# Hybrid mLSTM / sliding-window decoder layer: the forget gates' rows placed behind a branch gate's weights, and two value-projection weights whose remainders come from adding transfers

## The chip, the core and the metric

The kernel runs on one core of a Trainium2 chip. The metric is the device time of one execution in microseconds (us): the median of three runs was 878.63 us (878.37 to 880.06). One further execution was taken with the hardware profiler; all rows below come from it. Times inside the program are counted from the start of the profile's span.

The engines are named as the profile names them: PE is the matrix engine, PEld its weight load, DVE the vector engine, ACT the scalar engine, POOL the engine that here mostly issues transfers, SP the engine that issues most loads from memory. A row such as "L138 DVE TENSOR_TENSOR wl<-wr,wh" is an instruction of line 138 that reads the tiles wr and wh and writes the tile wl.

## The reference

One decoder layer over 512 tokens of width 1024, all in float32. What matters here is the first third of it:

```python
h = rmsnorm(x, norm_mix_g[i])
proj = h @ w_in[i]
qk_ml, v_ml, o_ml, if_pre, q_sw, k_sw, v_sw, g_a, g_b = jnp.split(proj, split_idx, axis=-1)
...
gates = (if_pre + b_if[i]).astype(jnp.float32)
ig = gates[..., :ML_HEADS]
lf = jax.nn.log_sigmoid(gates[..., ML_HEADS:])
h_ml = mlstm_chunkwise(q_ml, k_ml, v_ml.reshape(B, S, ML_HEADS, ML_DV), ig, lf)
...
y_a = jax.nn.sigmoid(o_ml) * h_ml
y_b = swa_with_sinks(...)
merged = jax.nn.sigmoid(g_a) * (y_a @ w_branch_a[i]) + jax.nn.sigmoid(g_b) * (y_b @ w_branch_b[i])
x = x + merged @ w_out[i]
```

A squared-ReLU MLP, a gated per-layer embedding and a last norm follow. `v_ml` is the value projection of the mLSTM, `o_ml` its output gate, `g_b` and `g_a` the two branch gates, `lf` the logarithm of the forget gates (four heads by 512 tokens), and `mlstm_chunkwise` runs over running sums and running maxima of `lf` and `ig`.

## The kernel before

**Two parts of each number.** A float32 operand of a matmul is split into a rounded part, `wh`, and a remainder, `wl`; a product is then three matmuls, written by `pairs` in the order high·high, high·low, low·high. For a weight this happens in `load_w`: a raw tile `wr` (128x1024, 512 KB) is cast by ACT to `wh` (L137) and DVE subtracts `wh` from `wr` into `wl` (L138). There are four buffers each for `wr`, `wh` and `wl`; a buffer of `wh` or `wl` comes free when PE has done the products of the weight four earlier, a buffer of `wr` when its last reader is done, and SP's next load into it waits for that. Where a later row of the projection's own raw tiles is not in `wr` it is in a tile called `wq`.

**Splitting by a transfer.** `split_by_transfer` does the same with DVE left out: ACT casts the high part (L145), ACT writes the negative of the rounded raw data into the low part's place through a scaled copy (L146), and POOL issues a transfer that adds the raw data onto it (L147). Before the change it is used only for sums of activations, tiles `hS`, 256 KB each.

**Seven products instead of eight.** Value projection, output gate and both branch gates are computed by `seven`, a scheme that forms a 2x2 block product from seven block products. Its products run in this order, with the results that each completes: p1, c11, t21, t22, c22, c12, c21. Before each, `form` splits a weight; some weights are first added to or subtracted from each other on DVE (L452, L453, L462, L466). `post` reads the accumulated result (ACT copies p1; DVE adds t21 and t22, at L515 or L646). In value projection and output gate (`by_tokens`) a product has two weights, 24 matmuls of 512 columns; in the branch gates (`gate_proj`, run twice for each gate, j = 0 and 1) it has one weight, 24 matmuls of 256 columns. Accumulators of a product pair are reused: t22 adds to t21's, so PE waits for DVE to have read t21; c11 adds to p1's, so PE waits for ACT's copy of p1.

**Order.** Every engine works through its own queue strictly in the order in which its instructions stand. Tile's scheduler merges the parts of the program into those queues by its own estimates; `tc.issue_after` and a few other calls hold a part behind a named instruction. The stages around the change are, in PE's order: value projection (44 to 83 us), output gate (83 to 122 us), first branch gate `w_gb` (122 to 164 us).

**The gates' rows.** `gates()` works on the four-partition rows of the input and forget gates: DVE L583, ACT exponential L584, ACT logarithm L585, DVE L586 together give `lf`; then a running maximum `mst` (L588), four running sums `fl` (L591), `rr` (L593), seven steps of `gg` (L600, L602), and one more exponential `em` on ACT (L604). The functions belong to different ACT tables, so table loads (ACT_TABLE_LOAD) stand between them. `gates` is called when the first branch gate's t22 is posted, but in the program as built L583 to L591 stand much earlier, within the value projection. The transposes of these rows (`gate_columns`) follow in the second half of the first branch gate.

Of the kernel before, what the change touches and what calls it, by code (L numbers as in the profile page):

```python
# [13 lines left out]
ALU = mybir.AluOpType  # L14
# [22 lines left out]
def block_kernel(  # L37
# [30 lines left out]
    V, A, G, T = nc.vector, nc.scalar, nc.gpsimd, nc.tensor  # L68
# [63 lines left out]
    last_low = [None]  # L132
# [19 lines left out]
        nc.sync.dma_start(out=raw[:, :n], in_=src)  # L152
        return raw

    def load_w(src, n, dims, raw=None, cast=False):

        if raw is None:
            raw = load_raw(src, n)
        parts = [wp.tile([P, 1024], F32R, tag=t, bufs=WB, name=nm(t))[:, :n] for t in ("wh", "wl")]
        if cast:  # L160
            nc.gpsimd.dma_start(out=parts[0], in_=src)
            last_low[0] = V.tensor_sub(parts[1], raw[:, :n], r32(parts[0]))
        else:
            split(parts, raw[:, :n])
        return [q.rearrange("p (k c) -> p k c", k=dims) for q in parts]

    def pairs(a, b):
# [215 lines left out]
    A11, A12, A22 = h_part(1, 1), h_part(1, 2), h_part(2, 2)  # L383
# [55 lines left out]
        S3.extend(h_split(s3))  # L439
        S4.extend(h_split(s4))  # L440

    def seven(form, prod, X, Y, Z, b, post, own_first=False):

        b11, b12, b21, b22 = b
        n = range(len(b11))
        for i in n:
            prod(X, A11, form(b11[i]), i, True)
        post("p1", X)  # L450
        for i in n:
            V.tensor_sub(b12[i], b22[i], b12[i])  # L452
            V.tensor_add(b11[i], b12[i], b11[i])  # L453
        for i in n:
            prod(X, A12, form(b21[i]), i, False, True)
        own = last_mm[0].ins
        if own_first:
            with tc.issue_after(last_low[0].ins):
                late_sums()
        post("c11", X)  # L460
        for i in n:
            V.tensor_sub(b21[i], b21[i], b11[i])  # L462
            w = form(b11[i])
            with tc.issue_after(own) if own_first else ExitStack():
                prod(Z, S2, w, i, True)
            V.tensor_sub(b11[i], b22[i], b11[i])  # L466
        post("t21", Z)
        for i in n:
            prod(Z, S1, form(b11[i]), i, False)
        post("t22", Z)  # L470
        for i in n:
            prod(Y, S3, form(b12[i]), i, True)
        post("c22", Y)
        for i in n:
            prod(Z, S4, form(b22[i]), i, False, True)
        post("c12", Z)
        for i in n:
            prod(Y, A22, form(b21[i]), i, False, True)
        post("c21", Y)


# [4 lines left out]
        vm.append(t)  # L486
    vld = dp.tile([P, NH, NT, DV], F32, name="vld")

    def by_tokens(w, post, own_first=False):

        raws = quads(w, ["wr", "wr", "lm", "lm", "wr", "wr", "lm", "lm"])
        b = ps_a()
        X, Y, Z = [ps_t(), ps_t()], [b[:, :512], b[:, 512:]], [ps_g(), ps_g()]

        def prod(ps, f, w, kh, first, last=False):
            for t in range(2):
                ops = []
                for k in range(2):
                    ops += pairs([h[:, t * P : (t + 1) * P] for h in f[2 * kh + k]], [h[:, k, :] for h in w])
                chain(ps[t], ops, first and kh == 0, last and kh == 1, True)  # L500

        seven(lambda r: load_w(None, 1024, 2, r), prod, X, Y, Z, [raws[2 * i : 2 * i + 2] for i in range(4)], post, own_first)

    def post_by_tokens(done):

# [40 lines left out]
    for m in range(NT):  # L546
        T.transpose(pgi[:4, m * P : (m + 1) * P], gt[:, m, :4], ident)
        T.transpose(pgf[:4, m * P : (m + 1) * P], gt[:, m, 4:], ident)
    by_tokens(w_vml, post_by_tokens(put_v), True)
    store_low()  # L550


# [27 lines left out]
    def gates():  # L580

        lf = row("lf")[:4, :]
        V.scalar_tensor_tensor(lf, fg, -1.0, fg, ALU.mult, ALU.max)  # L583
        A.activation(lf, lf, AF.Exp, scale=-1.0)  # L584
        A.activation(lf, lf, AF.Ln, bias=1.0)  # L585
        V.scalar_tensor_tensor(lf, fg, 0.0, lf, ALU.min, ALU.subtract)  # L586
        mst = act_f("mst")[:4, :]
        V.tensor_tensor_scan(mst, lf, ig, 0.0, ALU.add, ALU.max)  # L588
        fl = row("fl")[:4, :]
        for c in range(NT):  # L590
            V.tensor_tensor_scan(fl[:, c * P : (c + 1) * P], lf[:, c * P : (c + 1) * P], zeros4, 0.0, ALU.add, ALU.add)  # L591
        rr = act_f("rr")[:4, :]
        V.tensor_sub(rr, fl, mst)  # L593

        rrd = dp.tile([NH, 512], F32, name="rrd")
        nc.gpsimd.dma_start(out=rrd, in_=rr)
        gg = [act_f("gg")[:4, :] for _ in range(NT)]
        for t in range(NT):
            sl = slice(t * P, (t + 1) * P)
            V.tensor_sub(gg[t][:, sl], ig[:, sl], fl[:, sl])  # L600
            if t:
                V.tensor_scalar_add(gg[t][:, : t * P], gg[t - 1][:, : t * P], fl[:, t * P - 1 : t * P])  # L602
        em = act_f("em")[:4, :]
        A.activation(em, mst, AF.Exp, scale=-1.0)  # L604
        rows.extend(row("row") for _ in range(NH))
        for h in range(NH):
            nc.gpsimd.dma_start(out=rows[h], in_=rrd[h : h + 1, :].broadcast_to([P, 512]))
        rows_of_gates.extend((gg, em))
# [887 lines left out]
```

## Time and profile before

| | |
|---|---|
| median of three runs | 878.63 us |
| lowest and highest run | 878.37, 880.06 us |
| the profiled execution, its time | 878.13 us |
| its span, first to last instruction | 876.3 us |
| matmuls, whole span | 4428 |
| PE idle or late between 66 and 77 us / 77 and 89 / 124 and 137 / 137 and 151 | 0.00 / 0.35 / 0.42 / 0.00 us |
| bytes read from memory and written to it | 97.60 MB, 10.49 MB |

The row on idle time is the length of each stretch less PE's busy time in it. In a timeline a row gives start, duration, engine, line, operation, what is written and read, and in square brackets how long the engine was idle before it and what ended that. Rows of one line that follow each other directly are merged ("x2"): the start is that of the first. A duration includes the pipeline's end, so the next instruction can start a little before it is over.

### The profile page before, as it was taken

The page shows a single profiled execution, that of the slowest core. Times are in us where ns is not written, and L with a number is a line of the kernel's source. Part 1 is how long each engine was busy: PE and PEld are TensorE (multiplying, and loading weights), DVE is VectorE, ACT ScalarE, POOL GpSimd, SP SyncE. Part 2 cuts the span into 40 slices and gives each one's busy share as a digit, 9 for nine tenths or more (in the row PEclk, how much of TensorE's full clock was granted, in tenths as well). Part 3 has the DMA queues.
Part 4 walks back from the last instruction along what each step waited for, and adds up shares of the span by engine and source line. Part 5 has one row for each costly group of instructions (what it writes and reads, how often), then busy time and mean ns, then how long its engine had stood idle before and what let it go on. Part 6 is the DMA issues. An engine that isn't in the chain of part 4 may idle for free.

```text
span 876.3 us, 11735 instructions
## 1 busy us (share of the span) xinstructions
PE 864.2 (99%) x4428; PEld 727.1 (83%) x4428; DVE 671.5 (77%) x994; ACT 490.4 (56%) x826; POOL 43.7 (5%) x70
## 2 busy tenths in 40 slices
PE   9999999999999999999999999999999999999996
PEld 7888789998877778888888888888888888888886
DVE  6999889775788889777896669757956784698557
ACT  6685556444676568854344665356435634564843
POOL 1121111000000000000020000000000000020000
PEclk9999999999999999999999999999999999999999
DMA  8775246435121266664244612520452054125302
GB/s 268 209 185 207 97 148 209 146 115 202 49 97 50 72 231 215 209 254 148 73 88 148 222 47 73 204 106 4 135 178 73 0 192 145 49 54 139 120 1 96
DMA packets 35162, 115.14 MB, mean 131 GB/s; under 512 B 4893, under 2 KB 4893, under 8 KB 35106
## 3 DMA queue, kind: packets, MB, share of 16 engines
q1 hardware_dynamic: 28146, 95.25, 31.5%
q0 software_dynamic: 6816, 18.89, 7.9%
q8 instruction: 35, 0.57, 0.3%
q10 hardware_dynamic: 144, 0.26, 0.1%
q14 instruction: 21, 0.17, 0.1%
HBM read 97.60 MB, written 10.49 MB: 123 GB/s over the span
## 4 chain that ended last, share of the span: by engine, by line
PE 84%; DVE 7%; ACT 4%; DMA 3%; issue 2%; SPq 0%; ACTq 0%; DVEq 0%
PE psg L175 47%; PE psp L175 23%; PE psa L175 5%; DVE wl L138 2%; PE pst L175 2%; PE pst L778 1%; ACT wh L137 1%; DMA wr<-in_w_vsif 1%; DMA wq<-in_w_o 1%; ACT lm L743 1%; PE psa L720 1%; PE psa L859 1%; PE psa L881 1%; DVE qs L429 1%; PE psa L879 1%
## 5 line engine op out<-in xcount | busy, mean ns | idle before, releaser
L137 ACT CAST wh<-wr 128x1024 fp32r<-128x1024 f32 x130 | 136.5, 1052 | 159.4 <-PE psg L175 61.7
L138 DVE TENSOR_TENSOR wl<-wr,wh 128x1024 fp32r<-128x1024 f32 x130 | 158.1, 1219 | 79.9 <-ACT wh L137 78.9
L175 PE MATMUL psg<-x,wh 128*128 128x512 f32 x512 | 157.7, 389 | 0.0
L175 PE MATMUL psp<-wh,uf 128*128 128x512 f32 x448 | 138.5, 389 | 0.0
L175 PEld LDWEIGHTS psg<-x,wh 128*128 128x128 f32 x512 | 96.1, 188 | 19.9
L175 PE MATMUL psg<-x,wl 128*128 128x512 f32 x256 | 99.6, 389 | 0.0
L175 PEld LDWEIGHTS psp<-wh,uf 128*128 128x128 f32 x448 | 84.1, 188 | 17.4
L175 PE MATMUL psp<-wl,uf 128*128 128x512 f32 x224 | 87.1, 389 | 0.0
L175 PE MATMUL psg<-h,wh 128*128 128x512 f32 x256 | 80.9, 395 | 0.6 <-DVE rc L746 0.6
L137 ACT CAST wh<-wd 128x1024 fp32r<-128x1024 f32 x44 | 46.2, 1052 | 54.1 <-PE psp L175 21.9
L138 DVE TENSOR_TENSOR wl<-wd,wh 128x1024 fp32r<-128x1024 f32 x44 | 53.1, 1218 | 14.6 <-ACT wh L137 14.5
L175 PEld LDWEIGHTS psg<-x,wl 128*128 128x128 f32 x256 | 48.1, 188 | 9.9
L175 PEld LDWEIGHTS psg<-h,wh 128*128 128x128 f32 x256 | 46.9, 188 | 11.2 <-issue 1.6
L175 PE MATMUL psg<-h,wl 128*128 128x512 f32 x128 | 50.5, 395 | 0.0
L138 DVE TENSOR_TENSOR uf<-F,uf 128x1792 fp32r<-128x1792 f32 (+2 forms) x20 | 33.0, 1652 | 21.8 <-ACT uf L137 21.8
L175 PEld LDWEIGHTS psp<-wl,uf 128*128 128x128 f32 x224 | 42.1, 188 | 8.9
L175 PE MATMUL psg<-yb,wh 128*128 128x512 f32 x128 | 40.3, 393 | 0.0
L175 PE MATMUL psg<-ya,wh 128*128 128x512 f32 x128 | 39.9, 391 | 0.0
L137 ACT CAST uf<-F 128x1792 fp32r<-128x1792 f32 (+2 forms) x20 | 27.9, 1396 | 20.5 <-DVE F L1191 20.4
L1215 DVE SCALAR_TENSOR_TENSOR xk<-psp,r,xk 128x512 f32<-128x512 f32 x48 | 33.8, 744 | 5.5 <-PE psp L175 5.2
L175 PE MATMUL psg<-hS,wh 128*128 128x256 f32 x192 | 35.6, 285 | 0.2 <-DVE t L646 0.2
L175 PE MATMUL psa<-h,wh 128*128 128x256 f32 x192 | 35.4, 285 | 0.3 <-ACT p L656 0.2
(343 smaller groups left out, 1828.4 us busy)
## 6 DMA issues: line engine op xcount, KB each, us to landing
wr<-in_w_up SPq DMA_DIRECT2D x32, 512.0 KB, 3.3
wd<-in_w_down SPq DMA_DIRECT2D x24, 512.0 KB, 4.0
wr<-in_w_qsw SPq DMA_DIRECT2D x8, 512.0 KB, 4.2
gd<-gr POOLq DMA_DIRECT2D x8, 512.0 KB, 2.9
wr<-in_w_qkml SPq DMA_DIRECT2D x8, 512.0 KB, 3.2
wr<-in_w_b SPq DMA_DIRECT2D x8, 512.0 KB, 3.2
wh<-in_w_b POOLq DMA_DIRECT2D x8, 512.0 KB, 3.7
gl<-gd SPq DMA_DIRECT2D x8, 512.0 KB, 4.3
```

The costliest lines, as they stand in the source:

```text
L137: A.copy(dst[0], src)
L138: last_low[0] = V.tensor_sub(dst[1], src, r32(dst[0]))
L175: last_mm[0] = T.matmul(ps, l, r, start=first and i == 0, stop=last and i == len(ops) - 1, skip_group_check=parts)
L429: V.tensor_sub(t[o, :], ps[s, :], r32(t[s, :]))
L720: T.matmul(o, q[:, n * P : (n + 1) * P], kk[kp][ab][:, k0 : k0 + 256], start=True, stop=False)
L743: A.activation(lm3[:, g, :], lm3[:, g, :], AF.Exp, bias=nmx[:, g : g + 1], scale=0.125, accum_out=sm[:, g : g + 1])
L778: T.matmul(o[HALF[ab], :], v[:, c : c + 64], w[:, ab * 512 : (ab + 1) * 512], start=j == 0, stop=j == len(terms) - 1)
L859: T.matmul(psc[s], l, r, start=j == 0, stop=j == 2, skip_group_check=True)
L879: T.matmul(o, hi, vm[s][:, h, :], start=s == 0, stop=False, skip_group_check=True)
L881: last_mm[0] = T.matmul(o, lo, vm[s][:, h, :], start=False, stop=s == t, skip_group_check=True)
L1215: V.scalar_tensor_tensor(o, ps[:, t, :], r2[:, 2 * toks + t : 2 * toks + t + 1], o, ALU.mult, ALU.add)
```

## The change

`seven` gets a `last_form`, used for the two weights of its last product, c21; `by_tokens` makes it from a new argument `how`, and only the value projection passes one, `split_by_transfer`. `load_w` uses `how` in place of `split`. And the first instruction of `gates` is held behind `last_low[0]`, the subtraction that was recorded last when `gates` is called: that of the first branch gate's t22 weight.

```diff
-    def load_w(src, n, dims, raw=None, cast=False):
+    def load_w(src, n, dims, raw=None, cast=False, how=None):
...
-            split(parts, raw[:, :n])
+            (how or split)(parts, raw[:, :n])
...
-    def seven(form, prod, X, Y, Z, b, post, own_first=False):
+    def seven(form, prod, X, Y, Z, b, post, own_first=False, last_form=None):
...
         for i in n:
-            prod(Y, A22, form(b21[i]), i, False, True)
+            prod(Y, A22, (last_form or form)(b21[i]), i, False, True)
         post("c21", Y)
...
-    def by_tokens(w, post, own_first=False):
+    def by_tokens(w, post, own_first=False, how=None):
...
-        seven(lambda r: load_w(None, 1024, 2, r), prod, X, Y, Z, [raws[2 * i : 2 * i + 2] for i in range(4)], post, own_first)
+        seven(lambda r: load_w(None, 1024, 2, r), prod, X, Y, Z, [raws[2 * i : 2 * i + 2] for i in range(4)], post, own_first, lambda r: load_w(None, 1024, 2, r, how=how))
...
-    by_tokens(w_vml, post_by_tokens(put_v), True)
+    by_tokens(w_vml, post_by_tokens(put_v), True, split_by_transfer)
...
         lf = row("lf")[:4, :]
-        V.scalar_tensor_tensor(lf, fg, -1.0, fg, ALU.mult, ALU.max)
+        with tc.issue_after(last_low[0].ins):
+            V.scalar_tensor_tensor(lf, fg, -1.0, fg, ALU.mult, ALU.max)
```

One line is added in `gates`, so from there on a line of the changed kernel has a number higher by one (L583 becomes L584, L646 becomes L647), and the tiles' own numbers rise by two.

ACT's queue at the value projection's last weights, before (`wr_556` and `wr_558` are the two raw weights of c21, `vm` is a result):

```order
L137 CAST wh_792<-wq_560 128x1024
L137 CAST wh_808<-wq_562 128x1024
L137 CAST wh_834<-wr_556 128x1024
L137 CAST wh_850<-wr_558 128x1024
L540 CAST vm_530<-t_140_745 128x2x256
```

and now:

```order
L137 CAST wh_792<-wq_560 128x1024
L137 CAST wh_808<-wq_562 128x1024
L146 ACTIVATE wl_835<-wr_556 128x1024
L145 CAST wh_834<-wr_556 128x1024
L146 ACTIVATE wl_852<-wr_558 128x1024
L145 CAST wh_851<-wr_558 128x1024
L540 CAST vm_530<-t_140_745 128x2x256
```

Two instructions are added on ACT; DVE loses its two subtractions for these weights, and POOL gets two transfers, `wl_835<-wr_556` and `wl_852<-wr_558`, ahead of its third store of `vld`.

DVE's queue in the first branch gate, before, from the subtraction for the c12 weight (`wl_1379`) to that for the weight of the next half's p1 (`wl_1458`); the c21 weight is `wl_1410`:

```order
L138 TENSOR_TENSOR wl_1379<-wr_1178,wh_1378 128x1024
L646 TENSOR_TENSOR t_228_1277<-psg_1183,p_223_1214 128x256
L593 TENSOR_TENSOR rr_1320<-fl_1315,mst_1313 4x512
L600 TENSOR_TENSOR gg_1324<-ig_877,fl_1315 4x128
L600 TENSOR_TENSOR gg_1325<-ig_877,fl_1315 4x128
L602 TENSOR_SCALAR gg_1325<-gg_1324,fl_1315 4x128
L600 TENSOR_TENSOR gg_1326<-ig_877,fl_1315 4x128
L602 TENSOR_SCALAR gg_1326<-gg_1325,fl_1315 4x256
L600 TENSOR_TENSOR gg_1327<-ig_877,fl_1315 4x128
L602 TENSOR_SCALAR gg_1327<-gg_1326,fl_1315 4x384
L138 TENSOR_TENSOR wl_1410<-wr_1176,wh_1409 128x1024
L138 TENSOR_TENSOR wl_1458<-wq_1443,wh_1457 128x1024
```

Now, from the t22 weight (`wl_1283`) to `rr`; behind `rr` come the same seven rows of `gg`, then the subtractions `wl_1412` and `wl_1460` for the c21 weight and the next half's p1 weight:

```order
L138 TENSOR_TENSOR wl_1283<-wr_1174,wh_1282 128x1024
L584 SCALAR_TENSOR_TENSOR lf_1310<-fg_880 4x512
L138 TENSOR_TENSOR wl_1351<-wr_1176,wh_1350 128x1024
L647 TENSOR_TENSOR t_228_1279<-psg_1184,p_223_1216 128x256
L647 TENSOR_TENSOR t_228_1279<-psg_1185,p_223_1216 128x256
L452 TENSOR_TENSOR wq_1447<-wr_1451,wq_1447 128x1024
L587 SCALAR_TENSOR_TENSOR lf_1310<-fg_880,lf_1310 4x512
L589 SCALAR_TENSOR_TENSOR mst_1315<-lf_1310,ig_879 4x512
L592 SCALAR_TENSOR_TENSOR fl_1317<-lf_1310,zero_90 4x128 x4
L138 TENSOR_TENSOR wl_1381<-wr_1180,wh_1380 128x1024
L594 TENSOR_TENSOR rr_1322<-fl_1317,mst_1315 4x512
```

The whole chain of the rows now stands between the c22 weight (`wl_1351`) and the p1 weight (`wl_1460`), and L452, which before stood behind the p1 weight, stands in it as well; before, only `mst`, `rr` and `gg` stood here.

ACT's queue at the same place, now (before, L584 and L585 with their table loads stood in the value projection, and the casts of the c12, c21 and p1 weights followed that of the c22 weight with one sigmoid among them):

```order
L137 CAST wh_1282<-wr_1174 128x1024
L137 CAST wh_1350<-wr_1176 128x1024
L585 ACT_TABLE_LOAD
L585 ACTIVATE lf_1310<-lf_1310 4x512
L668 ACT_TABLE_LOAD
L668 ACTIVATE gr_1186<-psa_1182 128x2x256
L586 ACT_TABLE_LOAD
L586 ACTIVATE lf_1310<-lf_1310 4x512
L137 CAST wh_1380<-wr_1180 128x1024
L137 CAST wh_1411<-wr_1178 128x1024
L137 CAST wh_1459<-wq_1445 128x1024
```

Three table loads stand ahead of the c12 weight's cast, one of them more than the whole program had.

PE's queue where c22 of the first half ends, before (`psa_1181` is c22, `psa_1451` the next half's p1):

```order
L175 MATMUL psa_1181<-hS_652,wl_1349 128x256
L175 MATMUL psa_1451<-h_158,wh_1457 128x256
L175 MATMUL psa_1451<-h_159,wh_1457 128x256
L175 MATMUL psa_1451<-h_158,wl_1458 128x256
L175 MATMUL psa_1451<-h_158,wh_1457 128x256
```

and now (`psa_1183` is c22, `psa_1453` p1, `psg_1184` c12):

```order
L175 MATMUL psa_1183<-hS_652,wl_1351 128x256
L175 MATMUL psa_1453<-h_158,wh_1459 128x256
L175 MATMUL psa_1453<-h_159,wh_1459 128x256
L175 MATMUL psa_1453<-h_158,wl_1460 128x256
L175 MATMUL psg_1184<-hS_657,wh_1380 128x256
```

Three matmuls of the next half's p1, the third of which reads `wl_1460`, now stand ahead of c12; before it was 13 of them. The other 21 follow behind c21. SP's queue has the same order in both kernels.

## The prediction

> **What bounds the kernel now.** I read first the page's engine totals, then PE's timeline for places where a matmul comes late, then DVE's and ACT's timelines at the stages touched, to see how much room each has there.
>
> ```profile
> PE 864.2 (99%) x4428; PEld 727.1 (83%) x4428; DVE 671.5 (77%) x994; ACT 490.4 (56%) x826; POOL 43.7 (5%) x70
> 128.14:137.58 9.44, 9.23 (x77) 9.03 (x76) 9.26 (x17) 4.89 (x5) 1.34 (x3) 1.00 0.54 181
> ```
>
> PE bounds the whole: 864.2 of 876.3 us. The second row (stretch, length, then PE, PEld, DVE, ACT, POOL busy) is where the gates' rows are going: DVE is busy for 9.26 of 9.44 us there. Averaged over the span DVE has 23% free, but in this stretch 2%; so what is put there is delay for whatever stands behind it on DVE. PE's rows that matter:
>
> ```profile
> 77.61 0.39 PE L175 MATMUL psa<-wl,h 128*128 128x512 f32 x1
> 80.33 0.39 PE L175 MATMUL psa<-wl,h 128*128 128x512 f32 x1
> 88.03 0.61 PE L175 MATMUL pst<-wh,h 128*128 128x512 f32 x2
> 89.16 0.50 PE L175 MATMUL pst<-wl,h 128*128 128x512 f32 x1 [0.52 <-DVE wl L138]
> 137.46 0.28 PE L175 MATMUL psa<-h,wl 128*128 128x256 f32 x1
> ```
>
> 77.61 and 80.33 are the first uses of the two remainders that are now to come by transfer. At 89.16 PE really waits for DVE, in the output gate's c11. 137.46 is the third matmul of the first branch gate's second p1, the first that reads its remainder. It starts without a wait, 0.24 us after DVE delivered that remainder (the row 136.01 below).
>
> **The value projection's weights.** DVE loses two subtractions, and the early gate work:
>
> ```profile
> 54.43 0.68 DVE L583 SCALAR_TENSOR_TENSOR lf<-fg 4x512 f32<-4x512 f32 x1
> 56.12 1.23 DVE L138 TENSOR_TENSOR wl<-wr,wh 128x1024 fp32r<-128x1024 f32 x1 [0.26 <-ACT wh L137]
> 67.55 0.67 DVE L586 SCALAR_TENSOR_TENSOR lf<-fg,lf 4x512 f32<-4x512 f32 x1
> 69.29 1.35 DVE L591 TENSOR_TENSOR_SCAN fl<-lf,zero 4x128 f32<-4x128 f32 x4
> 72.73 1.22 DVE L452 TENSOR_TENSOR wq<-wq,wq 128x1024 f32<-128x1024 f32 x1 [0.97 <-DMA wq<-in_w_o]
> 75.07 1.21 DVE L138 TENSOR_TENSOR wl<-wr,wh 128x1024 fp32r<-128x1024 f32 x1
> 87.89 2.35 DVE L138 TENSOR_TENSOR wl<-wr,wh 128x1024 fp32r<-128x1024 f32 x2
> 69.42 1.05 ACT L137 CAST wh<-wr 128x1024 fp32r<-128x1024 f32 x1 [1.67 <-PE psa L175]
> 72.14 1.06 ACT L137 CAST wh<-wr 128x1024 fp32r<-128x1024 f32 x1 [1.67 <-PE psa L175]
> ```
>
> The row at 87.89 delivers, with the first of its two, the remainder for which PE waits at 89.16. In the new order it stands ahead of the second L453 and of two L541, and one subtraction (75.07) fewer stands in front of it in a stretch in which DVE never idles, so it is at least 2 us earlier. That wait goes: the matmul starts 0.91 us after the one before it (the second of the pair from 88.03, 0.61 less 0.39 behind the first), where the pace is 0.22: **-0.7**. The gate rows that leave this stage save nothing by themselves, because DVE waits behind them anyway, at 56.12 for ACT and at 72.73 for a load.
>
> Will the transfers be in time? Nearest rows are the adding transfers of half the size:
>
> ```profile
> 51.84 0.84 POOL L147 DMA_DIRECT2D hS<-s  x1 [13.05 <-ACT hS L146]
> hS<-s POOLq DMA_DIRECT2D x4, 256.0 KB, 3.9
> GB/s 0 0 0 0 0 0 0 0 0 0 0 0 8 221 213 188 213 188 58 205 180 213 205 188 107 213 172 221 188 205 189 213 205 188 164 312 311 279 164 279
> 71.79 4.86 SPq L185 DMA_DIRECT2D wr<-in_w_o  x2
> ```
>
> Four of 256 KB ran at about 200 GB/s (third row, 50 to 60 us) with 3.9 us from issue to landing. 512 KB take 1.3 us more, 5.2. ACT's scaled copies start at 69.42 and 72.14 (PE frees the buffers then) and take about 1.05 each, so the issues are at 70.8 and 73.5. The first lands at about 76.0, 1.6 ahead of 77.61. The second moves its data behind the first and lands between 78.5 and 80.8, against 80.33: a stall of 0 to 0.5, and I take 0. SP's two loads into the same raw buffers (71.79) are issued only on those landings, some 4 us later. Their casts stood at 81 and 83 us behind PE's release of the buffers, so that costs nothing while they land by 84.
>
> **The gates' rows.** What they add lies on DVE and ACT between the c22 weight and the second p1 weight. All times are on the clock of before; the 0.7 gained comes off at the end, since DVE's chain here hangs on PE's results.
>
> ```profile
> 126.14 2.00 ACT L137 CAST wh<-wr 128x1024 fp32r<-128x1024 f32 x2
> 57.54 1.28 ACT L584 ACT_TABLE_LOAD   x1
> 58.83 0.63 ACT L584 ACTIVATE lf<-lf 4x512 f32<-4x512 f32 x1
> 59.37 1.04 ACT L137 CAST wh<-wr 128x1024 fp32r<-128x1024 f32 x1
> 130.15 0.59 ACT L667 ACTIVATE gr<-psa 128x512 f32<-128x512 f32 x1
> ```
>
> ACT: two casts until 128.14; a load and an exponential 1.83 (57.54 to 59.37), until 130.0; a load and the sigmoid 1.28 + 0.59, until 131.85; the third load and the logarithm 1.91: **133.8**.
>
> The Trainium skill ("ScalarE: Activation LUTs", What ACT_TABLE_LOAD costs) adds about 1.38 us of drain to each load of 1.28. By that rule the logarithm would be ready 4.1 us later. The rows above leave no room for it: the load starts 0.02 after a cast's end, and 0.01 lies between load and activation.
>
> ```profile
> 127.22 2.36 DVE L138 TENSOR_TENSOR wl<-wr,wh 128x1024 fp32r<-128x1024 f32 x2 [1.17 <-ACT wh L137]
> 129.76 0.43 DVE L646 TENSOR_TENSOR t<-psg,p 128x256 f32<-128x256 f32 x1 [0.18 <-PE psg L175]
> 130.10 1.20 DVE L588 TENSOR_TENSOR_SCAN mst<-lf,ig 4x512 f32<-4x512 f32 x1
> 131.23 1.19 DVE L138 TENSOR_TENSOR wl<-wr,wh 128x1024 fp32r<-128x1024 f32 x1
> 132.35 0.41 DVE L646 TENSOR_TENSOR t<-psg,p 128x256 f32<-128x256 f32 x1
> 132.68 0.67 DVE L593 TENSOR_TENSOR rr<-fl,mst 4x512 f32<-4x512 f32 x1
> ...
> 134.88 1.21 DVE L138 TENSOR_TENSOR wl<-wr,wh 128x1024 fp32r<-128x1024 f32 x1
> 136.01 1.21 DVE L138 TENSOR_TENSOR wl<-wq,wh 128x1024 fp32r<-128x1024 f32 x1
> 137.15 1.21 DVE L452 TENSOR_TENSOR wq<-wr,wq 128x1024 f32<-128x1024 f32 x1
> 128.47 1.46 SPq L185 DMA_DIRECT2D wr<-in_w_gb  x2
> wr<-in_w_gb SPq DMA_DIRECT2D x2, 512.0 KB, 4.1
> ```
>
> DVE: `lf` (0.65) stands between the two subtractions of 127.22, so the second ends at 130.2 instead of 129.6, and SP's second load (the row 128.47; its second issue is 0.33 before 129.93) goes out at 130.2. L452 needs that load. It lands 3.2 (the shortest landing of a `w_gb` weight) to 4.1 (the row) later, at 133.4 to 134.3; I take 133.6, because the two issues are now further apart. Both L646 are done by then. From 133.6, each at its distance to the next: L452 1.15, second `lf` 0.6, `mst` 1.13, `fl` 1.28, c12 subtraction 1.13, `rr` and `gg` 2.2 (132.68 to 134.88), c21 subtraction 1.13, p1 subtraction 1.21. That ends at **143.4**. PE has been standing at the p1's third matmul since 137.46: 6.0 late. Less the 0.7 already gained, PE is at +5.3.
>
> Queued behind that matmul is all of PE. c12 must also wait until DVE has read t22, which is next in DVE's queue: 0.34 later, 0.14 of it covered by the p1 matmul, **+0.2**. Then the second p1 ends only after c21, and ACT's copy of it now stands behind a sigmoid and a cast that waits for the same p1:
>
> ```profile
> 146.19 0.59 ACT L656 COPY p<-psa 128x512 f32<-128x512 f32 x1
> ```
>
> The cast (1.05), the copy and the two handovers make 1.8 to 2.1 after p1's end; PE has 13 matmuls of t21 at 0.12, 1.56, to do meanwhile. I take **+0.6**, bounds 0.2 and 1.0.
>
> Sum: -0.7 + 6.0 + 0.2 + 0.6 = **+6.1**. Against the profiled execution, 878.13, that is 884.2 (span 882.4, with the same 1.8 around it). The median of the runs before lies 0.5 above the profiled one, so the time predicted is **884.7**.
>
> Bounds of the unknown costs: if L452's load is already there, the logarithm is what DVE waits for and the remainder comes at 142.6, -0.8; the copy at its low end, -0.4; the 0.2 falls away: +4.7 in all. If the load takes 4.1, +0.7; the copy at its high end, +0.4; the transfers stall c21 by 0.5 and the late loads keep the wait at 89.16, +1.2: +8.4. The forecast's own range is 883.3 to 887.0.
>
> **Rivals.**
>
> *The rows fit in, and only the gain stays* (7%). DVE would have to deliver the p1 remainder by 136.8. For: 9.3 us lie between the c22 cast's end (128.14) and that matmul, and DVE is not full before them. Against: what now stands on DVE from 128.4 on adds up to 12.3 us with no wait at all (0.65 + 1.13 + 2 x 0.34 + 1.15 + 0.6 + 1.13 + 1.28 + 1.13 + 2.2 + 1.13 + 1.21), so even with every input ready it would end at 140.7. Time: 878.6 - 0.7, less 0.3 for the t22 wait (132.35) that the new order removes: 877.6. It decides only if some row on DVE is far cheaper than on the clock of before.
>
> *The stall is there and is partly won back* (9%). For: during it SP's loads run on and ACT idles. Against: behind it PE is busy nearly all the time, so there is hardly a wait left to shrink. 2 to 4 us would be left: 880.6 to 882.6.
>
> *The transfers are late* (12%). For: the output gate's loads still move when the first is issued (one lands at 72.73), and the second has no slack at its late end. PE would wait in c21, and the late raw tiles keep the wait at 89.16: 0.5 + 0.7 on top, 885.9; with double the wait 886.4.
>
> *A switch of tables costs ACT more than its row* (4%). Were each of the three worth two loads, 1.28 more, the logarithm would come at 137.6 in place of 133.8, and DVE's second `lf`, at 134.75 in the sum, 2.9 later: 887.6. The three rows above speak against it, but there each load stood alone. With the drain on the Trainium skill's page named above it would be 887.9.
>
> *The forecast* has the remaining 68%.
>
> **How the numbers follow.** The first rival makes the kernel faster (7%); a won-back stall that leaves nothing visible, 2%, makes it the same; all else is slower, 91%. About 0.2%, 1.8 us, is what a measurement of this kernel can tell from no change. The range: the forecast's 883.3 to 887.0, extended down to 881.6 for the upper half of the won-back case; that leaves out the first rival, half of the second, the drains and the forecast's tails.
>
> **What would show it.** Right: PE's timeline has one gap of 5 to 7 us near 137 us, at a matmul `psa<-h,wl`, ended by DVE wl L138; DVE between 130 and 143 us holds L452, both scans, `rr` and `gg` in front of that subtraction; L452 waits for a `w_gb` load; no gap near 89 us; no gap near 80 us; a small one in front of the second half's c11. Wrong: no gap near 137 us, a first gap at 77 or 80 us that ends on a transfer, or a gap of over 1 us between a table load and an activation that is ready. If PE's gap is there but the whole is less than 3 us slower, I missed a place where the time comes back.

## The result, and the profile after

| | before | changed |
|---|---|---|
| median of five runs each | 878.52 us | 889.41 us |
| lowest and highest | 878.37, 880.06 | 888.24, 890.19 |
| the profiled execution, its span | 878.13, 876.3 | 889.41, 887.6 |
| mean granted TensorE clock | 0.998 | 0.993 |

The changed kernel is slower by a ratio of 1.0121 (95% interval 1.0110 to 1.0133); that is 10.6 us by the ratio, 10.9 between the medians. The prediction was 884.7, at most 887.0: the sign and the place were right, the size was not. In the changed kernel all lines from `gates` on stand one further (L583 is now L584, L587 is the second `lf`, L594 `rr`, L605 `em`, L647 the reading of t22).

PE's timeline of the changed kernel at the places that the prediction speaks of (start, duration, operation, idle time before it and what ended that):

```profile
89.09 0.50 PE L175 MATMUL pst<-wh,h 128*128 128x512 f32 x1 [0.64 <-ACT p L512]
...
137.24 0.28 PE L175 MATMUL psa<-hS,wl 128*128 128x256 f32 x1
137.43 0.50 PE L175 MATMUL psa<-h,wh 128*128 128x256 f32 x2
145.16 0.58 PE L175 MATMUL psa<-h,wl 128*128 128x256 f32 x1 [7.24 <-DVE wl L138]
146.59 0.80 PE L175 MATMUL psg<-hS,wh 128*128 128x256 f32 x2 [0.84 <-DVE t L647]
...
158.51 0.28 PE L175 MATMUL psg<-hS,wh 128*128 128x256 f32 x1
158.79 0.50 PE L175 MATMUL psa<-h,wh 128*128 128x256 f32 x2
```

The last matmul of c22 starts at 137.24; before it was 137.10 (the first row below). So PE enters this place 0.1 late. It then stands at the third matmul of p1 until 145.16: the pair at 137.43 is over at 137.93, 7.24 us are idle, and 7.5 are lost against the pace of 0.12 a matmul. It stands a second time at c12's first matmul, which starts 1.43 behind the one before it, 1.3 beyond the pace. At 158.79, c11, 0.16 is lost.

The same places in the kernel before, from PE's timeline: c22's last matmul and c12's first.

```profile
137.10 0.28 PE L175 MATMUL psa<-hS,wl 128*128 128x256 f32 x1
...
138.78 0.49 PE L175 MATMUL psg<-hS,wh 128*128 128x256 f32 x2
```

Now the windows of the changed kernel (stretch, length, busy time and count of PE, PEld, DVE, ACT, POOL, then the granted clock, DMA share, GB/s):

```profile
128.00:137.30 9.30, 9.30 (x80) 9.30 (x78) 5.61 (x8) 9.21 (x10) 0.00 (x0) 1.00 0.42 141
137.30:145.10 7.80, 0.63 (x4) 0.31 (x3) 7.80 (x16) 2.06 (x3) 1.26 (x3) 0.75 0.21 75
145.10:146.50 1.40, 0.58 (x1) 0.29 (x1) 0.40 (x3) 1.37 (x3) 1.40 (x3) 0.50 0.95 354
146.50:151.60 5.10, 5.01 (x24) 5.01 (x25) 4.70 (x7) 1.51 (x2) 0.03 (x1) 0.52 0.64 206
151.60:157.00 5.40, 5.40 (x48) 5.40 (x47) 3.91 (x5) 3.09 (x4) 0.54 (x1) 1.00 0.24 97
```

The page's first row and its row of granted clocks, in 40 slices:

```profile
PE 867.1 (98%) x4428; PEld 729.2 (82%) x4428; DVE 669.8 (75%) x992; ACT 493.6 (56%) x829; POOL 45.6 (5%) x72
PEclk9999997999999999999999999999999999999999
```

The clock is the part that the prediction did not have. It falls to 0.50 while PE stands (the 7 among the slices), and c12's 24 matmuls take 5.1 us, where the next stretch does 48 in 5.4. PE counts as fully busy there, so neither the list of gaps nor PE's share of 98% shows it; only the clock and the count beside the busy time do.

### The profile page after: what moved, and what is told of

Read it like the earlier page. It is cut to its first block, busy times and chain, and to the rows that moved or that the text cites. A ratio compares the mean times of both kernels' runs of the same rounds, so it can differ in the third digit from the quotient of the medians.

```text
span 887.6 us, 11742 instructions
## 1 busy us (share of the span) xinstructions
PE 867.1 (98%) x4428; PEld 729.2 (82%) x4428; DVE 669.8 (75%) x992; ACT 493.6 (56%) x829; POOL 45.6 (5%) x72
## 4 chain that ended last, share of the span: by engine, by line
PE 83%; issue 9%; DVE 3%; ACT 3%; POOL 2%; DMA 0%; POOLq 0%; ACTq 0%; DVEq 0%
PE psg L175 46%; PE psp L175 23%; PE psa L175 4%; PE pst L779 1%; PE pst L175 1%; PE psa L721 1%; PE psa L722 1%; POOL vld L526 1%; PE psa L860 1%; PE psa L882 1%; PE psa L880 1%; PE psa L881 1%; PE psg L267 1%; POOL god L569 1%; PE psa L758 1%
## 5 line engine op out<-in xcount | busy, mean ns | idle before, releaser
L137 ACT CAST wh<-wr 128x1024 fp32r<-128x1024 f32 x128 | 134.4, 1052 | 162.4 <-PE psg L175 60.4
L138 DVE TENSOR_TENSOR wl<-wr,wh 128x1024 fp32r<-128x1024 f32 x128 | 155.7, 1219 | 80.8 <-ACT wh L137 79.8
L175 PEld LDWEIGHTS psg<-h,wh 128*128 128x128 f32 x256 | 46.9, 188 | 11.2 <-issue 1.6
L175 PE MATMUL psg<-hS,wh 128*128 128x256 f32 x192 | 37.7, 295 | 0.8 <-DVE t L647 0.8
```

The costliest lines, as they stand in the source:

```text
L137: A.copy(dst[0], src)
L138: last_low[0] = V.tensor_sub(dst[1], src, r32(dst[0]))
L175: last_mm[0] = T.matmul(ps, l, r, start=first and i == 0, stop=last and i == len(ops) - 1, skip_group_check=parts)
```

## The experiments

Each kernel was timed in five rounds beside runs of the kernel before on the same chip. Ratios are to those.

| run | median us | ratio (95% interval) |
|---|---|---|
| changed kernel | 889.41 | 1.0121 (1.0110 to 1.0133) |
| tie only | 889.09 | 1.0123 (1.0109 to 1.0136) |
| transfers only | 878.93 | 1.0007 (0.9998 to 1.0015) |
| PE busy through the wait | 887.51 | 1.0100 (1.0084 to 1.0115) |
| em's buffer asked for early | 888.97 | 1.0118 (1.0105 to 1.0132) |
| em in place of mst | 888.33 | 1.0113 (1.0099 to 1.0127) |
| both: PE busy, em in place | 886.96 | 1.0096 (1.0082 to 1.0110) |
| L452 behind the rows | 887.34 | 1.0096 (1.0082 to 1.0110) |
| rows behind p1's weight | 885.24 | 1.0078 (1.0064 to 1.0092) |
| rows at the first half's p1 | 884.29 | 1.0067 (1.0054 to 1.0080) |
| rows behind both gates | 878.06 | 0.9999 (0.9991 to 1.0008) |
| the same, without transfers | 877.24 | 0.9991 (0.9982 to 1.0000) |
| one transfer only | 878.68 | 1.0007 (0.9998 to 1.0016) |

**Which half of the change.** Tie alone, against the changed kernel:

```diff
-    by_tokens(w_vml, post_by_tokens(put_v), True, split_by_transfer)
+    by_tokens(w_vml, post_by_tokens(put_v), True)
```

> The kernel before with the tie alone; the two remainders stay DVE subtractions. Theory (the tie makes the whole loss): PE waits 6 to 8 us at the third matmul of w_gb's second p1 for its remainder, c12 waits about 1.3 us more, c12's matmuls run at half clock; the whole is 10 to 12 us slower than before, 888.5 to 890.5, ratio 1.0115 to 1.0135. Rival (the two transfers push the loads behind them back and so carry 1 us or more of the loss, through the late w_gb load that L452 waits for): 886.5 to 888, the w_gb load issued at 130.2 in place of 130.81.

Transfers alone:

```diff
-        with tc.issue_after(last_low[0].ins):
-            V.scalar_tensor_tensor(lf, fg, -1.0, fg, ALU.mult, ALU.max)
+        V.scalar_tensor_tensor(lf, fg, -1.0, fg, ALU.mult, ALU.max)
```

> The two remainders by transfer alone; the gates' rows stay where they were. Theory (the wait at 89 us of the output gate's c11 only changes hands, from DVE's subtraction to ACT's copies of p1, so the transfers bring nothing): within 0.7 us of before, 878 to 879.2. Rival A (with DVE freed the wait goes): 0.7 faster, 877.8. Rival B (the early gate rows are still on DVE and ACT here, so the transfers start later and PE waits for them in c21): a gap near 78 or 80 us and 879.5 or more.

The tie carries all of the loss that can be measured, the transfers none. PE's timeline with the tie only shows the two waits of the changed kernel over again:

```profile
144.68 0.58 PE L175 MATMUL psa<-h,wl 128*128 128x256 f32 x1 [7.21 <-DVE wl L138]
146.09 0.80 PE L175 MATMUL psg<-hS,wh 128*128 128x256 f32 x2 [0.82 <-DVE t L647]
```

In that trace the `w_gb` load goes out some 0.5 us sooner than in the changed kernel, which was the rival's sign, and both waits come 0.5 us sooner; but the time, 889.09, is not the rival's 886.5 to 888. With the transfers only, the wait at 89 us has changed hands as the theory had it: PE waits for ACT's copy of p1 (PE's timeline of that run).

```profile
88.70 0.50 PE L175 MATMUL pst<-wh,h 128*128 128x512 f32 x1 [0.27 <-ACT p L512]
```

**Is it the clock?** 74 matmuls are put on PE into an unused bank, ahead of c12; the scheduler moves the three first matmuls of p1 behind c21.

```diff
+    def keep_busy():
+        pk = ps_t()
+        with tc.issue_after(last_mm[0].ins):
+            for _ in range(74):
+                T.matmul(pk[:, :256], A22[0][0][:, :P], A22[0][0], start=True, stop=True, skip_group_check=True)
...
-    gbd = gate_proj(w_gb, {(0, "t22"): [gates], (1, "c11"): [gate_columns]})
+    gbd = gate_proj(w_gb, {(0, "t22"): [gates], (0, "c22"): [keep_busy], (1, "c11"): [gate_columns]})
```

> The changed kernel, with 74 matmuls of 128 x 256 put on PE ahead of c12 into an unused bank, so that PE works through the wait; their result is read by nobody. At 0.115 us each they fill about 8.5 us, 137.3 to 145.9; the second p1's first three matmuls go behind c21. Theory (2.2 us of the loss are PE's clock, which halves while PE stands): c12 still starts at about 146.6, since DVE's rows set that, its 24 matmuls take 2.8 us in place of 5.0 at a granted clock near 1.0, and the whole is 2.0 to 2.5 us below the changed kernel: 886.9 to 887.4, ratio to before 1.0093 to 1.010. Rival (the matmuls after the wait are slow for another reason, such as the operands just written): c12 takes 5 us again and the time stays at 889 to 890.

It came out at 887.51, just above the 886.9 to 887.4 expected, and c12 still starts at 146.39 (before this edit 146.59). PE's timeline and windows of this run:

```profile
136.87 9.04 PE L690 MATMUL pst<-h 128*128 128x256 f32 x74
146.39 0.51 PE L175 MATMUL psg<-hS,wh 128*128 128x256 f32 x2 [0.49 <-DVE t L647]
...
136.80:145.70 8.90, 8.90 (x76) 8.90 (x75) 7.88 (x16) 2.85 (x4) 2.06 (x4) 1.00 0.32 103
146.30:149.30 3.00, 2.91 (x24) 2.91 (x25) 3.00 (x5) 1.51 (x2) 0.04 (x1) 1.00 0.77 218
```

The 24 matmuls take 3.0 us at a clock of 1.00 instead of 5.1 at 0.52. Work that nobody reads makes the kernel about 1.9 us faster than the changed one (its slowest run, 887.78, is below the changed kernel's fastest, 888.24), though three matmuls of p1, 0.36 us, now follow later. So about 2 us of the loss are the clock and not the wait.

**What holds c12?** In the changed kernel DVE's t22 read comes 1 us after the p1 remainder, behind ACT, which waits for a transfer (DVE's and then ACT's timeline):

```profile
143.90 1.21 DVE L138 TENSOR_TENSOR wl<-wq,wh 128x1024 fp32r<-128x1024 f32 x1
146.11 0.76 DVE L647 TENSOR_TENSOR t<-psg,p 128x256 f32<-128x256 f32 x2 [1.00 <-ACT em L605]
...
144.16 1.28 ACT L605 ACT_TABLE_LOAD   x1 [5.67 <-DMA rrd<-rr]
145.45 0.63 ACT L605 ACTIVATE em<-mst 4x512 f32<-4x512 f32 x1
```

POOL issues that store (POOL's timeline), and it lands 2.6 us later, just before 144.16:

```profile
141.54 0.54 POOL L597 DMA_DIRECT2D rrd<-rr  x1 [14.23 <-DVE gg L601]
```

Nothing that `em` computes needs the store of `rr`; a shared buffer would make it wait. First try, the buffer asked for earlier in the program:

```diff
         mst = act_f("mst")[:4, :]
+        em = act_f("em")[:4, :]
...
-        em = act_f("em")[:4, :]
```

> The changed kernel, with the buffer of em taken before rr's instead of behind it, so that it is not rr's own. Theory (c12's wait is a chain of buffers: rr's store of 2.6 us to DRAM, then em in rr's buffer, then t22 in the buffer of mst, which em reads): ACT's load of the exponential's table no longer waits 5.67 us for that store, L647 follows the p1 subtraction at once, c12's first matmul comes 0.9 to 1.1 us sooner, and the whole is about 1.0 below the changed kernel: 888.2 to 888.6. Rival (DVE's rows or ACT's next table load set c12's start anyway): L647 still ends at 146.4 and the time stays at 889 to 890.

It failed: the load of the table still waits 5.65 us for the same store, and the time is that of the changed kernel. By that wait, asking earlier did not change which buffer is given. Second try, no buffer at all:

```diff
-        em = act_f("em")[:4, :]
+        em = mst
```

> The changed kernel, with em written over mst in place, so that it needs no buffer of its own. The run with em's buffer asked for earlier left the wait as it was, so the buffer is given at the first write and not where the program asks for it: em still got rr's. Theory (rr's store, em in rr's buffer, t22 in mst's): the table load at 144.16 no longer waits 5.67 us for the store, em is done by about 143.2, L647 follows the p1 subtraction at 145.1, c12's first matmul comes at about 145.6 in place of 146.59, and the whole is 0.9 to 1.1 us below the changed kernel, 888.0 to 888.5. Rival (t22 then takes rr's buffer and waits for the store's landing itself, later than 145.1): c12 stays at 146 to 146.6, no gain.

ACT and PE in that run:

```profile
138.29 1.28 ACT L605 ACT_TABLE_LOAD   x1
140.85 0.63 ACT L605 ACTIVATE mst<-mst 4x512 f32<-4x512 f32 x1 [1.27 <-DVE rr L594]
...
144.74 0.58 PE L175 MATMUL psa<-h,wl 128*128 128x256 f32 x1 [7.03 <-DVE wl L138]
145.12 0.76 PE L175 MATMUL psg<-hS,wh 128*128 128x256 f32 x2
```

The wait at c12 is gone: it starts 0.38 behind the p1 matmul instead of 1.43. That a shared buffer made it is thereby shown; that it was `rr`'s is read from the releaser in the rows above. Why DVE's reading of t22 waits for `em` at all (by the expectation, because its result takes the buffer of `mst`) was not tested by itself. The total went down by about 0.7 to 1.1 (ratios 1.0121 and 1.0113, medians 889.41 and 888.33), the expected size, though the two intervals overlap, and the size is in part luck: c12 came 1.47 sooner, 0.42 of it because the p1 remainder did, and the span is only 0.9 shorter, because the clock in that trace came back 5.9 us after c12's start and not 4.8. The two repairs together, with 65 matmuls:

> em in place of mst, and 65 matmuls on PE through the wait (74 in the run before). Theory (terms add): c12 starts at about 145.5 and its 24 matmuls take 2.8 us: 0.9 to 1.1 below the run with 74 matmuls, 886.4 to 886.6, ratio to before about 1.009; what is left is the wait for DVE's rows, some 8.3 us between c22's last matmul and c12's first. Rival (c12's start hangs on something else behind em): no less than 887.3.

886.96 is 0.4 to 0.6 above what was expected, and 0.55 below the run with 74 matmuls, half of the sum. In its trace c12 starts at 145.36, 1.0 sooner than there, as expected; the spans, 885.7 and 884.9, differ by 0.8. The difference of the medians is within the spread of such runs.

**How long is DVE's chain, and where does it start?** L452 of the second half, which waits for its load, is put behind the rows.

```diff
-            V.tensor_sub(b12[i], b22[i], b12[i])
+            with tc.issue_after(behind[0]) if behind[0] else ExitStack():
+                V.tensor_sub(b12[i], b22[i], b12[i])
...
-                V.tensor_scalar_add(gg[t][:, : t * P], gg[t - 1][:, : t * P], fl[:, t * P - 1 : t * P])
+                behind[0] = V.tensor_scalar_add(gg[t][:, : t * P], gg[t - 1][:, : t * P], fl[:, t * P - 1 : t * P]).ins
```

> The changed kernel, with L452 of the second half, which waits for the w_gb load until 135.2, put behind the gates' rows on DVE. Theory (the chain to PE's wait starts at that load's landing, and the logarithm is ready at 134.54): the second lf starts at 134.6 in place of 136.34, everything behind it comes 1.7 earlier, PE's wait is 5.5 in place of 7.24 and still long enough to halve the clock; the whole is 1.7 below the changed kernel, 887.5 to 888.0, ratio about 1.0103. Rival (what is queued behind L452, the weights of the second half's c11 and t21, is late in its place): 888.8 or more, with a gap ahead of the second half's c11 or t21.

First the chain of the changed kernel, then that of this run (DVE's timelines; here the lines stand two to three further, L589 is the second `lf`), with PE's wait:

```profile
135.20 1.23 DVE L452 TENSOR_TENSOR wq<-wr,wq 128x1024 f32<-128x1024 f32 x1 [2.97 <-DMA wr<-in_w_gb]
136.34 0.67 DVE L587 SCALAR_TENSOR_TENSOR lf<-fg,lf 4x512 f32<-4x512 f32 x1
```

```profile
133.73 0.68 DVE L589 SCALAR_TENSOR_TENSOR lf<-fg,lf 4x512 f32<-4x512 f32 x1 [2.33 <-ACT lf L588]
...
142.55 0.58 PE L176 MATMUL psa<-h,wl 128*128 128x256 f32 x1 [5.47 <-DVE wl L139]
```

PE's wait falls by 1.77, from 7.24 to 5.47; 1.74 was expected. ACT's logarithm has become what DVE waits for. The total, 887.34, is 2.1 below the changed kernel, just below the 887.5 to 888.0 expected; its profiled execution is the fastest of its four runs, 885.78, so from it only the wait itself is read.

**Does the place make the price?** Three other places for the same rows, and the last one with the two subtractions back on DVE.

```diff
-    gbd = gate_proj(w_gb, {(0, "t22"): [gates], (1, "c11"): [gate_columns]})
+    gbd = gate_proj(w_gb, {(1, "p1"): [gates], (1, "c22"): [gate_columns]})
```

> The changed kernel, with the gates' rows called at the second half's p1, so tied behind that p1's own weight and not ahead of it, and the transposes of their columns at the second half's c22. Theory (it is the place that costs, since the rows stand on DVE ahead of the remainder that PE needs next): no gap over 1 us near 137 to 146, the remainder wl of p1 ends by 138; what is lost comes later and is smaller, because ACT's copy of p1 now stands behind em and so behind the scans: a gap of 1 to 4 us ahead of the second half's c11; in all 880 to 884. Rival (the rows cost their own length wherever they stand while PE has no slack): 887 or more.

```diff
-    gbd = gate_proj(w_gb, {(0, "t22"): [gates], (1, "c11"): [gate_columns]})
+    gbd = gate_proj(w_gb, {(0, "p1"): [gates], (1, "c11"): [gate_columns]})
```

> The changed kernel, with the gates' rows called at the first half's p1 of w_gb, one stage earlier, so that the scans stand on DVE ahead of t21's and c22's weights. DVE has about 1.2 us free between 118 and 128 us there and the rows with their two waits on ACT take 7.5. Theory (the rows cost their length less what DVE has free until the next weight that PE needs): no wait near 145, but one of 3 to 6 us near 127 to 132, at a matmul of the first half's t21 or c22, without a long enough stand to halve the clock; 881 to 885. Rival (as cheap as in the stage of the value projection, where the rows cost nothing): 878 to 879.5.

```diff
-    gbd = gate_proj(w_gb, {(0, "t22"): [gates], (1, "c11"): [gate_columns]})
+    gbd = gate_proj(w_gb)
     gad = gate_proj(w_ga)
...
+    gates()
     for i in range(1, 4):
         q_proj(i)
+    gate_columns()
```

> The changed kernel, with the gates' rows called behind the second branch gate (w_ga) and their columns behind the query projections that follow. The rows are first read at 318 us in the trace of before, and between 190 and 220 us DVE is busy there for 15.8 of 30. Theory (the rows cost PE only where DVE has nothing free ahead of the next weight): no gap over 0.6 us from 100 to 250 us, granted clock 0.998 as before; 877.4 to 878.6, so within 0.2% of before or just under it. Rival (a tie behind a weight costs something wherever it stands, in ACT's table loads and in the copies behind them): 880 or more.

And the same, with the value projection's line as in the run with the tie only:

> The same place of the rows, with the value projection's two remainders back on DVE as before. Theory (the transfers bring nothing): within 0.5 us of the run with transfers, 877.4 to 878.6. Rival (with the rows out of the way the transfers do shorten the wait at 89 us): 0.5 to 1.0 slower than that run.

The first two move the loss and don't remove it. PE's timelines, of the rows behind p1's weight and of those at the first half's p1:

```profile
147.54 0.74 PE L175 MATMUL psg<-hS,wh 128*128 128x256 f32 x4 [1.61 <-ACT wh L137]
151.33 0.58 PE L175 MATMUL psg<-hS,wl 128*128 128x256 f32 x1 [3.05 <-DVE wl L138]
```

```profile
129.48 0.58 PE L175 MATMUL psg<-hS,wl 128*128 128x256 f32 x1 [3.89 <-DVE wl L138]
```

Behind p1's weight the gap near 145 is gone, as expected, but 885.24 is above the 880 to 884 given: PE stands in t21 of the second half, first for ACT's cast, which is now behind table loads, and then for the next remainder behind the scans. I had named c11 and ACT's copy of p1; that was the wrong place. At the first half's p1 the one wait came where and as large as expected and 884.29 is in the range, but the clock was halved after it all the same, which I had ruled out (windows of that run):

```profile
125.20:129.40 4.20, 0.39 (x4) 0.19 (x2) 4.20 (x9) 1.51 (x3) 1.42 (x2) 0.91 0.31 126
129.40:133.80 4.40, 4.32 (x20) 4.32 (x21) 3.69 (x11) 3.10 (x5) 1.98 (x4) 0.50 0.04 12
```

Behind both gates the rows cost nothing that can be measured: 878.06. The windows say why. In this stretch, first of the kernel before and then with the rows there and no transfers, DVE has room and PE has no idle time in either:

```profile
190.00:220.00 30.00, 30.00 (x195) 27.42 (x194) 15.75 (x20) 12.37 (x16) 1.06 (x2) 1.00 0.49 168
```

```profile
190.00:220.00 30.00, 30.00 (x187) 26.82 (x186) 21.26 (x34) 20.71 (x24) 3.74 (x7) 1.00 0.59 197
```

The trace of the run with the transfers, whose profiled execution is the slowest of its eleven, does have two waits over the 0.6 us that were expected at most: 0.91 at 182.27 for DVE and 0.80 at 190.61 for ACT's copy. Both come before the rows, whose first instruction stands at 197.73, so the rows did not make them.

The same rows, tied in the same way, so cost 10.9, 6.6, 5.6 or 0 us (medians) in the four places. What DVE has free differs between the first and the last of them: in the kernel before it is 0.18 of 9.44 us in the prediction's stretch from 128.14 to 137.58, and 14.25 of 30 us here; for the two between, that it is DVE's and ACT's free time that sets the price is argued from the waits above. Without the transfers this place gives 877.24, at a ratio of 0.9991 (0.9982 to 1.0000), the fastest version found, though it is at the edge of what can be told from the kernel before. It is 0.8 faster than with the transfers, where theory said within 0.5 and the rival slower: neither came, and as the two intervals overlap, it is not shown that the transfers cost anything.

**The wait at 89 us.** Only the first of the two remainders by transfer, against the transfers alone:

```diff
-... lambda r: load_w(None, 1024, 2, r, how=how))
+... lambda r: load_w(None, 1024, 2, r, how=how if r is raws[4] else None))
```

> The transfers alone, but only for the first of the two remainders; the second is a DVE subtraction again, and the gates' rows stay where they were. Theory (the second transfer holds its raw buffer 5.6 us, so the w_o load into that buffer lands at 83.7, ACT's cast and DVE's rows behind it come 0.7 to 1.3 us later and ACT's copies of p1 take over the wait at 89 us): the second w_o load is issued by about 78 and lands by 82.5, the cast behind it starts at 83.1 without waiting for a transfer, PE's gap near 88 to 89 us is under 0.4 us over the pace; 877.8 to 878.5. Rival (the order of the copies behind the casts makes that wait, whenever the load lands): the gap stays at 0.5 to 0.7 and is still ended by ACT's copy of p1.

The theory fell. The second load did come earlier and ACT's cast started at 83.06 without waiting for a transfer, and the gap was still there, ended by ACT's copy (PE's timeline of that run):

```profile
88.76 0.50 PE L175 MATMUL pst<-wh,h 128*128 128x512 f32 x1 [0.34 <-ACT p L512]
```

So it is not the late load. What is left is the new order on DVE: the two additions L539 that ACT's casts L540 wait for, and with them the cast and the copies queued behind, start later than before, behind two L453 in a row. DVE's timeline of this run, then of the kernel before:

```profile
83.07 2.35 DVE L453 TENSOR_TENSOR wr<-wq,wr 128x1024 f32<-128x1024 f32 x2
85.34 1.27 DVE L539 TENSOR_TENSOR t<-psa,t 128x512 f32<-128x512 f32 x2
```

```profile
83.22 1.22 DVE L452 TENSOR_TENSOR wq<-wq,wq 128x1024 f32<-128x1024 f32 x1
84.35 1.28 DVE L539 TENSOR_TENSOR t<-psa,t 128x512 f32<-128x512 f32 x2
```

That this order alone makes the gap was not tried.

## Why the prediction was wrong in size, step by step

In us, against the sum of the prediction; measured values from the timelines and windows above. The places add to 11.2, the spans differ by 11.3, and the sum was 6.1. In the prediction's own terms four steps failed: "That wait goes" was worth nothing, "I take 133.6" for the load's landing was too early, "+0.2" for c12 left out a second condition, and c12's matmuls were put at the old pace without a term for the clock.

| step | predicted | measured |
|---|---|---|
| wait at 89 us gone, PE's lead at c22's end | -0.7 | +0.1 |
| stand at p1's third matmul | +6.0 | +7.5 |
| c12 waits for t22's reading | +0.2 | +1.3 |
| c12's 24 matmuls at half the clock | not in the sum | +2.1 |
| ACT's copy ahead of c11 | +0.6 | +0.2 |

**"That wait goes: -0.7".** It failed. The remainder on DVE did come earlier, done at 84.6 where it had been 89.1, but I priced DVE alone. ACT's copies of p1, which c11 also needs, were then last. The run with one transfer shows that the landing of the loads, which the prediction held against 84 us and which came at 83.7, is not the reason. PE was 0.6 late at the first half's c11 (126.71, before 126.11) and 0.1 late at c22's end, mainly because its wait of 0.21 at 132.81 in the kernel before is gone.

**The transfers.** Right in the main: they landed 5.8 and 5.6 us after their issue, with no gap at 77 or 80 us. "5.2" was a little low.

**The stand at p1.** Mechanism, instruction and releaser as predicted; what was too small in the term is the load's landing. From L452's start to the remainder's end I had 9.8, and the rows say 9.9 (135.20 to 145.11). But L452 started at 135.20, not at 133.6. SP's second load went out at 130.8 (the row below, less its issue of 0.33) where I had 130.2, since DVE and ACT run 0.6 late here, where the prediction had them 0.7 early (the t22 subtraction stands at 127.83, before at 127.22). And the load landed 4.3 after its issue, where "I take 133.6" stood for 3.4. SP's timeline and the issues of that stretch:

```profile
129.08 2.05 SPq L185 DMA_DIRECT2D wr<-in_w_gb  x2
...
wr<-in_w_gb SPq DMA_DIRECT2D x1, 512.0 KB, 4.3
```

The nearest row, 4.1, had been the upper bound; it was closer than the value taken. The run with L452 behind the rows shows that what L452 adds behind the logarithm counts in full: 0.66 of wait for the load and its own 1.14, together 1.80, and PE's wait fell by 1.77. ACT's side held: the logarithm was done at 134.54 (ACT's timeline below) for 133.8 on the clock of before, and 0.60 of the difference is that its two casts start later, at 126.74 for 126.14.

```profile
133.91 0.63 ACT L586 ACTIVATE lf<-lf 4x512 f32<-4x512 f32 x1
```

**c12, "+0.2".** The step took DVE's queue as all that stands between p1 and t22's reading. `em` in the buffer of `rr`, whose store takes 2.6 us, was the second condition. It could be read before the change: there ACT's table load waits for the same store, and DVE's reading starts only 0.04 after `em` ends, with L452 between it and the p1 remainder (ACT's and DVE's timelines of before).

```profile
136.34 1.28 ACT L604 ACT_TABLE_LOAD   x1 [0.86 <-DMA rrd<-rr]
137.63 0.63 ACT L604 ACTIVATE em<-mst 4x512 f32<-4x512 f32 x1
...
138.30 0.76 DVE L646 TENSOR_TENSOR t<-psg,p 128x256 f32<-128x256 f32 x2
```

But in the kernel before PE had 13 matmuls of p1, 1.6 us, to do ahead of c12, and now it has three.

**The clock.** Not in the sum, and the largest single omission. In the kernel before no wait of PE between 60 and 240 us is over 0.52 us and the clock is 1.00 there, so its trace could not show it. The Trainium skill ("TensorE: Matmul & The Clock Gate", Part 1: The HAM clock gate) states it: after at least one idle window of about 3.4 us the PE clock goes to half, and comes back after at least one busy window of about the same length. The trace is near that for the fall (3.3 us, last section). By that page, after a stand of 6 us, c12's matmuls take twice 0.12 for one window, some 14 of the 24, and the forecast would have been at least 1.7 higher, 886.4, an estimate; were all 24 that slow, as the trace has nearly all of them, 2.9 higher. What the runs show is +2.1.

**"+0.6" for the copy ahead of c11.** Too high; 0.16 was lost. The mechanism was right: p1's last matmul was over at 157.23, ACT's cast stood at 157.20 and its copy ended at 158.74, and c11 started at 158.79, so the chain took 1.6 where the step had 1.8 to 2.1.

**The rivals.** Rows that fit in, a stall won back, and late transfers did not come. Nor did dearer table switches: each of the three loads took 1.28 and the activation started 0.01 to 0.02 behind it, so the drain of 1.38 that the Trainium skill ("ScalarE: Activation LUTs", What ACT_TABLE_LOAD costs) adds is not seen here either. Nothing was won back at the end: PE was 11.3 behind at c11 and is 11.3 behind at the last instruction.

## What to carry to other kernels

Where PE sets the time, work on another engine has no price of its own: the same rows cost from 0 to 10.9 us by their place, so read what that engine has free before the next thing that PE needs from a window of the place and not from the share over the span. A predicted long stand of PE needs a second term, for the matmuls behind it at half the clock: here stands of 3.9 us and more halved it. And a wait that goes is worth only what the next condition of the same matmul leaves: list all of them, buffers too, with the time at which each is met.

## What the hardware showed that I had not expected

PE's clock against time, in the changed kernel (windows):

```profile
140.00:141.00 1.00, 0.00 (x0) 0.00 (x0) 1.00 (x2) 0.00 (x0) 0.00 (x0) 1.00 0.00 0
141.00:142.00 1.00, 0.00 (x0) 0.00 (x0) 1.00 (x6) 0.00 (x0) 0.46 (x1) 0.59 0.21 41
...
150.00:151.00 1.00, 1.00 (x6) 1.00 (x6) 1.00 (x2) 0.00 (x0) 0.00 (x0) 0.50 0.29 111
151.00:151.60 0.60, 0.60 (x6) 0.60 (x5) 0.20 (x1) 0.00 (x0) 0.00 (x0) 0.66 0.00 0
```

A mean of 0.59 between 1.00 and 0.50 puts the drop at about 141.2, some 3.3 us after PE's last matmul was over (137.43 + 0.50). It is back at about 151.4, 4.8 us after c12 began and 6.2 after the single matmul at 145.16. Read from windows in the same way, the fall came 3.1 us after the last matmul in the run with `em` in place and in that with the rows at the first half's p1, and the return 5.9 and 6.0 us after the matmuls began. By that the fall comes a little before the about 3.4 us of the Trainium skill ("TensorE: Matmul & The Clock Gate", Part 1: The HAM clock gate). The page calls the window free-running and asks for at least one, so a return after 4.8 to 6.0 us is not against it. A stand of 3.89 us was enough in the run with the rows at the first half's p1, and so were 1.61 and 3.05 with four matmuls between them in the run with the rows behind p1's weight, whose window behind them reads:

```profile
151.20:156.40 5.20, 5.07 (x24) 5.08 (x25) 3.66 (x4) 2.00 (x2) 1.80 (x4) 0.51 0.67 221
```

There the clock fell at about 149.5, 1.2 us after those four matmuls and 3.6 after the first stand began: a few matmuls in a stand did not keep the clock.

Transfers that add, 512 KB within on-chip memory (the issues of the changed kernel between 70 and 74 us):

```profile
wl<-wr POOLq DMA_DIRECT2D x2, 512.0 KB, 5.7
```

Plain transfers of that size have medians from 3.1 to 7.2 us in that kernel's list of issues, so this is not outside them. The raw buffer that such a transfer reads stays taken for those 5.7 us, which a subtraction of 1.2 us on DVE doesn't ask for, and with or without the tie no pair of runs shows a gain from them: 1.0121 with and 1.0123 without, 1.0007 against 1, 0.9999 against 0.9991.
